# Value projection for two head pairs per pass, 512 weight columns into four PSUM banks, in a transformer block on one Trainium2 core

## The chip, the core and the metric

The kernel runs on one core of one Trainium2 chip, as one launch. Its time is the device time of an execution in microseconds (us). Five engines work side by side, each through its own instruction stream in a fixed order: TensorE (PE, matrix products into the PSUM banks; its weight loads are shown apart as PEld), VectorE (DVE), ScalarE (ACT), GpSimd (POOL) and SyncE (SP, which issues DMA transfers here). A wait between engines is a wait on a semaphore. PSUM is used here as eight banks, each of 512 float32 numbers in each of 128 partitions.

## The reference

One transformer block on x with 512 rows of 2048 float32 numbers:

```
h    = rmsnorm(x, g_attn)
proj = h @ w_in                    # 2048 x 6152: q, k, v of 8 + 8 heads of width 128, and 8 forget logits
o_sb  = stick_breaking_attention(8 heads, strictly causal)
o_fox = forgetting_attention(8 heads, causal softmax with a cumulative log-forget bias)
x = x + concat(head_rmsnorm(o_sb), head_rmsnorm(o_fox)) @ w_out
x = x + relu(rmsnorm(x) @ w_up)**2 @ w_down
y = rmsnorm(x)
```

The change touches only how the values v (two times 8 heads of 128 columns of `proj`) are projected and where some temporaries of the head norm of the second last head and of the last head lie.

## The kernel before, in words

**Three products for one.** Every float32 operand is split into a rounded high part and the remainder: `split` (L57) lets ACT write the high part (L59, or L62 with a scale) and DVE the low part (L60, L63). `mm3` (L82 to L85) then does three PE matmuls for each product: high times high, high times low, low times high.

**Weights.** `load_w` (L70) brings a tile of 1024 columns per partition (512 KB) from HBM by one DMA on SP's queue (L73), into one of three `wraw` buffers, and splits it with one ACT cast (L59) and one DVE subtraction (L60) into `wh` and `wl`, three buffers of each.

**Order of the heads.** `order` holds the heads in pairs: forgetting ("fox") heads 6, 7, then 0 to 5, then stick-breaking ("sb") heads 0 to 7. The loop over n = 0, 2, ..., 14 takes one pair each time. It projects q and k of both heads (`project_q`: 48 matmuls of 512 columns each into one bank of the pool `acc`, tile `accq`), then, from n = 2 on, the values of the pair (`accumulate_v`), and then it attends with both heads. The values of the first pair come out of the stage before, together with the forget logits (264 columns).

**Values.** `accumulate_v` (L152) holds the normalized input hH/hL still (128 rows of x by 128 channels) and moves the weight columns past it. For a pair these are m = 256 columns, so that two of the four row groups t share a bank of 512: two `accv` banks of the pool `acc`, which has four. A weight tile holds four groups of 128 channels (there are 16, counted by k); for each t and each k there are three matmuls 256 columns wide: 16 x 4 x 3 = 192 for a pair. `take_v` (L172) scales and splits the sums into `vh` and `vl`: for each t one ACT (L62) and one DVE instruction (L63) of 128x256.

**Attention.** PSUM gives three banks to the tile `s`/`pt` and one to `o`, `ck`, `ssq`, both single, so heads follow one another. A fox head: `ck` (a matmul, L271) and its ACT copy `cb`, scores `s` on PE, additions into `w` on DVE (L277), causal mask on POOL, row maxima on DVE (L282), Exp on ACT (L285), scaling on DVE (L288), then `pt`: ten PE transposes of `w` (L218). `weigh` (L213) splits `pt` into `ph` and `pl` (one buffer of each), multiplies them with the values into `o`, and takes the norm over the head width: the square sum goes through PE (`ssq`), the rest through DVE and ACT, with `ph` and `pl` again as scratch (`n1`, `n2`); the result is written to `mixed` (L251). The next head's `ph` and `pl` have to wait until the norm of the head before has ended. The last head (`last=True`) has six scratch tiles of its own (`os_last`, `sq_last`, ...) and its `o` and square sum (`oq`) in the three-bank tile.

**After the attention.** The output projection (`acco`, its transposes in L424) goes over the heads in the same order of pairs, k0 = 0 to 14, in four blocks of 512 output columns with four banks each, so that the pair of the last two heads is what its first block needs last. Then come the up and down projections (`accu`, `accd`), which the change leaves as they are.

**Who sets the order.** The program text is rearranged by a scheduler: each engine gets one fixed list of instructions, with the attention of a head at high priority and the projections as what fills PE between its steps. So the order of the changed kernel can be read before it has run.

Of the kernel before, what the change touches and what calls it, by code (L numbers as in the profile page):

```python
# [8 lines left out]
F32 = mybir.dt.float32  # L9
F32R = mybir.dt.float32r  # L10
# [4 lines left out]
P = 128  # L15
NT = 512
TB = NT // P
D = 2048
KC = D // P
NH = 8  # L20
# [16 lines left out]
def block_kernel(ctx, tc, x, g_attn, w_in, b_f, g_out_sb, g_out_fox, w_out, g_mlp, w_up, w_down, g_final, y):  # L37
    nc = tc.nc
    pe, act, dve, pool, sp = nc.tensor, nc.scalar, nc.vector, nc.gpsimd, nc.sync
# [3 lines left out]
    w_in, w_out, w_up, w_down = w_in[0], w_out[0], w_up[0], w_down[0]  # L43
# [9 lines left out]
    acc = ctx.enter_context(tc.tile_pool(name="acc", bufs=4, space=PSUM))  # L53
# [3 lines left out]
    def split(hi, lo, src, scale=None):  # L57
        if scale is None:
            ins = act.copy(hi, src)  # L59
            lows[0] = dve.tensor_tensor(lo, src, hi.bitcast(F32), op=ALU.subtract)  # L60
        else:
            ins = act.mul(hi, src, scale)  # L62
            dve.scalar_tensor_tensor(lo, src, scale, hi.bitcast(F32), op0=ALU.mult, op1=ALU.subtract)  # L63
        return ins
# [5 lines left out]
    def load_w(src, a, b):  # L70

        raw = wp.tile([P, a, b], F32, tag="wraw", name="wraw")
        sp.dma_start(raw, src)  # L73
        out = []
        per = min(a, 2 * NT // b)
        for i in range(0, a, per):
            hi, lo = (w.rearrange("p (a b) -> p a b", a=per) for w in hi_lo(per * b))
            split(hi, lo, raw[:, i:i + per, :])
            out += [(hi[:, j, :], lo[:, j, :]) for j in range(per)]
        return out  # L80
# [42 lines left out]
    g_up, g_sb, g_fx = g_rest[:, :KC], g_rest[:, KC:KC + NH], g_rest[:, KC + NH:]  # L123
# [10 lines left out]
    with (  # L134
# [17 lines left out]
        def accumulate_v(c0, m, steps, prepare=None, more=None):  # L152

            per = NT // m
            banks = [acc.tile([P, NT], F32, tag="acc", name="accv") for _ in range(2)]
            if more is not None:
                banks += [more.tile([P, NT], F32, tag="more", name="accm") for _ in range(2)]
            ps = [banks[t // per][:, t % per * m:(t % per + 1) * m] for t in range(TB)]
            k1 = 0
            for step in steps:  # L160
                k0, k1 = k1, k1 + step
                if prepare is not None:
                    prepare(k0, step)
                w = load_w(w_in[k0 * P:(k0 + step) * P, c0:c0 + m].rearrange("(a p) c -> p a c", p=P), step, m)
                for t in range(TB):
                    ts = slice(t * P, (t + 1) * P)
                    for i in range(step):
                        k = k0 + i
                        mm3(ps[t], hH[:, k, ts], hL[:, k, ts], *w[i], k == 0 and t % per == 0, k == KC - 1)
            return ps  # L170

        def take_v(ps):  # L172
            vh = at.tile([P, TB, 2 * P], F32R, tag="vh", name="vh", bufs=2)
            vl = at.tile([P, TB, 2 * P], F32R, tag="vl", name="vl", bufs=2)
            for t in range(TB):
                split(vh[:, t, :], vl[:, t, :], ps[t][:, :2 * P], r1[:, t:t + 1])
            return vh, vl

        def project_q(c0, c, rb):
            ps = acc.tile([P, NT], F32, tag="acc", name="accq")  # L180
# [12 lines left out]
        def wide(name, dt=F32):  # L193
            return at.tile([P, 1280], dt, tag=name, name=name)
# [9 lines left out]
        def rows(w):  # L204
            return [w[:, OFF_Q[i]:OFF_Q[i] + (i + 1) * P] for i in range(TB)]
# [4 lines left out]
                pool.affine_select(out=d, in_=d, compare_op=op, fill=fill, base=0,  # L210
                                   pattern=[[0, n], [-1, P]] if n > 1 else [[-1, P]], channel_multiplier=1)

        def weigh(h, v, hc, w, gv, last=False):  # L213

            pt = atp.tile([P, 1536], F32, tag="s", name="pt")
            for j in range(TB):
                for i in range(j, TB):
                    pe.transpose(pt[:, OFF_T[j] + (i - j) * P:OFF_T[j] + (i - j + 1) * P],  # L218
                                 w[:, OFF_Q[i] + j * P:OFF_Q[i] + (j + 1) * P], ident)
            ph, pl = wide("ph", F32R), wide("pl", F32R)  # L220
            split(ph, pl, pt[:, :1280])
            hs = slice(hc * P, (hc + 1) * P)
            if last:
                oq = atp.tile([P, 1536], F32, tag="s", name="oq")
                o, q = oq[:, :NT], oq[:, NT:2 * NT]
            else:
                o = atp.tile([P, NT], F32, tag="o", name="o")
            for j in range(TB):
                n = NT - j * P
                js = slice(OFF_T[j], OFF_T[j] + n)  # L230
                mm3(o[:, j * P:], v[0][:, j, hs], v[1][:, j, hs], ph[:, js], pl[:, js], j == 0, j == TB - 1)
            if last:
                os_, sq, va, ra = (at.tile([P, NT], F32, name=f"{c}_last") for c in ("os", "sq", "va", "ra"))
                sh, sl = (at.tile([P, NT], F32R, name=f"{c}_last") for c in ("sh", "sl"))
            else:
                os_ = up.tile([P, NT], F32, tag="ul4", name="os")
                ra = up.tile([P, NT], F32, tag="uh5", name="ra")
                n1, n2 = wide("ph"), wide("pl", F32R)
                sq, va = n1[:, :NT], n1[:, NT:2 * NT]
                sh, sl = n2[:, :NT], n2[:, NT:2 * NT]  # L240
                q = None
            act.copy(os_, o)
            dve.tensor_tensor(sq, os_, os_, op=ALU.mult)
            split(sh, sl, sq)
            if q is None:
                q = atp.tile([P, NT], F32, tag="o", name="ssq")
            pe.matmul(q, onesr, sh, start=True, stop=False)
            pe.matmul(q, onesr, sl, start=False, stop=True)
            dve.tensor_scalar(va, q, 1.0 / P, EPS, op0=ALU.mult, op1=ALU.add)
            rsqrt(va, va, ra, sq)  # L250
            dve.scalar_tensor_tensor(mixed[:, h, :], os_, gv, va, op0=ALU.mult, op1=ALU.mult)  # L251

        def attend_sb(h, v, hc, q, k):
            s = scores(q, k)
            w = wide("w")
            act.activation(w, s, AF.Abs)
            act.activation(w, w, AF.Exp, scale=-1.0)
            act.activation(w, w, AF.Ln, bias=1.0)
            dve.scalar_tensor_tensor(w, s, 0.0, w, op0=ALU.max, op1=ALU.add)
            causal(w, ALU.is_gt, 0.0)  # L260
            for r in rows(w):

                dve.tensor_tensor_scan(r[:, ::-1], r[:, ::-1], r[:, ::-1], 0.0, op0=ALU.add, op1=ALU.max)
            dve.tensor_tensor(w, s, w, op=ALU.subtract)
            act.activation(w, w, AF.Exp)
            causal(w, ALU.is_gt, 0.0)
            weigh(h, v, hc, w, g_sb[:, h:h + 1], h == order[-1])

        def attend_fox(h, v, hc, q, k):
            ck = atp.tile([P, NT], F32, tag="o", name="ck")  # L270
# [21 lines left out]
        order = [NH + h for h in (6, 7, 0, 1, 2, 3, 4, 5)] + list(range(NH))  # L292

        def v_columns(h):
            return 2 * WSB + h * P if h < NH else o0 + 2 * WSB + (h - NH) * P

        with tc.tile_pool(name="tr0", bufs=2, space=PSUM) as trp:
# [30 lines left out]
                            junk = wide("ph")[:, :2 * NT].rearrange("p (a b) -> p a b", a=2)  # L328
                            act.activation(junk, xb[:, c:c + 2, t, :], AF.Square, accum_out=ss1[:, t, k // 8:k // 8 + 1])

            ps = accumulate_v(v_columns(order[0]), 2 * P + NH, [1, 1] + [2] * 7, prepare, trp)
            column_vectors(g_rest, *(g[0].rearrange("(h p) -> h p", p=P) for g in (g_mlp, g_out_sb, g_out_fox)))
            act.dma_start(bf, b_f.to_broadcast([P, NH]))
            r1 = row_rstd(ss1, "r1")
# [22 lines left out]
        with tc.tile_pool(name="attp", bufs=1, space=PSUM) as atp:  # L357
# [6 lines left out]
            fe = at.tile([P, TB, NH], F32, name="fe")  # L364
            for t in range(TB):
                dve.scalar_tensor_tensor(fl[:, t, :], ps[t][:, 2 * P:], r1[:, t:t + 1], bf, op0=ALU.mult, op1=ALU.add)
            v = take_v(ps)
            act.activation(fe, fl, AF.Abs)
            act.activation(fe, fe, AF.Exp, scale=-1.0)
            act.activation(fe, fe, AF.Ln, bias=1.0)  # L370
# [18 lines left out]
            for n in range(0, 2 * NH, 2):  # L389
                def project(i):  # L390
                    h = order[n + i]
                    e = (o0 if h >= NH else 0) + h % NH * P
                    return project_q(e, 2 * i, rbq), project_q(e + WSB, 2 * i + 1, rb)

                def attend(i, qk):
                    h = order[n + i]
                    with tc.high_priority():
                        (attend_fox if h >= NH else attend_sb)(h % NH, v, i, *qk)

                qk = [project(0), project(1)]  # L400
                if n:
                    v = take_v(accumulate_v(v_columns(order[n]), 2 * P, [4] * 4))
                for i in range(2):
                    attend(i, qk[i])

# [7 lines left out]
    trp = trp_cm.__enter__()  # L413
# [14 lines left out]
    for n in range(4):  # L428
        ns = slice(n * NT, (n + 1) * NT)
        ps = [acc.tile([P, NT], F32, tag="acc", name="acco") for _ in range(TB)]  # L430
        for k0 in range(0, 2 * NH, 2):
            e0 = order[k0]
            w = load_w(w_out[e0 * P:(e0 + 2) * P, ns].rearrange("(a p) c -> p a c", p=P), 2, NT)
# [141 lines left out]
    for g in range(NG):  # L575
        for db in range(2):
# [5 lines left out]
            b = load_b(g, db)  # L582
            for j, p in enumerate(ORDER):
                if j in steps:
                    job.step()
                w = b_form(p, b)
# [89 lines left out]
    banks = [(acc, "acc"), (tps, "tps")]  # L676
# [39 lines left out]
```

## Time and profile before

| | |
|---|---|
| median of 3 runs | 2152.41 us (2151.77 to 2153.89) |
| the profiled execution: its time | 2151.46 us |
| the profiled execution: its span (first to last instruction) | 2149.4 us |
| busy PE, PEld, DVE, ACT, POOL | 2131.2, 1801.0, 1402.8, 881.0, 63.2 us |
| granted TensorE clock over the span | 0.998 |

The profile shows one execution. Lines such as L83 are lines of the kernel before. A group row gives line, engine, operation, written tile <- read tiles, shapes and count, then busy time, the mean duration of one in ns, and the idle time of the engine ahead of them with what ended most of it. Matmuls overlap: one of 512 columns is shown as some 390 ns long while the next starts after some 230 ns, so a time for PE is taken from start to start (called the pitch here) and not from the duration. A timeline row gives start and duration in us; in square brackets stands the idle time of the engine before it and what ended that. A window row gives the length of the stretch and the busy time of the engines in it with the count of instructions.

### The profile page before, as it was taken

How to read it: one execution, taken by the hardware profiler on the slowest of the kernel's cores; microseconds unless marked ns; L12 is line 12 of the kernel's file. 1: busy time of each engine (PE TensorE's matmuls, PEld its weight loads, DVE VectorE, ACT ScalarE, POOL GpSimd, SP SyncE). 2: the span in 40 equal slices, each digit the busy share in tenths (PEclk: the TensorE clock that was granted, in tenths of full speed). 3: DMA queues.
4: the chain of work that ended last, by engine and by line, in shares of the span. 5: the costliest groups of instructions: out<-in, count | busy, mean ns of one | idle time of the engine just before them, and what ended most of it. 6: DMA issues, size and time to landing. Idle time of an engine off the chain costs nothing.

```text
span 2149.4 us, 25658 instructions
## 1 busy us (share of the span) xinstructions
PE 2131.2 (99%) x10356; PEld 1801.0 (84%) x10356; DVE 1402.8 (65%) x1547; ACT 881.0 (41%) x1146; POOL 63.2 (3%) x75
## 2 busy tenths in 40 slices
PE   9999999999999999999999999999999999999997
PEld 8888988998997888888888888888888888888886
DVE  5455555766566554566776776766776776777788
ACT  6333333444345445443433333333433433433444
POOL 0000000000010000000000000000000000000005
PEclk9999999999999999999999999999999999999999
DMA  6333333322333324233333233233233233233323
GB/s 189 80 84 83 78 83 84 79 79 79 89 112 123 94 93 157 69 118 98 98 114 102 89 117 108 89 114 112 88 108 118 88 99 120 87 101 120 92 70 127
DMA packets 201366, 216.71 MB, mean 101 GB/s; under 512 B 6768, under 2 KB 156832, under 8 KB 201120
## 3 DMA queue, kind: packets, MB, share of 16 engines
q1 hardware_dynamic: 200288, 212.95, 32.9%
q10 hardware_dynamic: 960, 2.13, 0.3%
q8 instruction: 81, 1.33, 0.3%
q14 instruction: 37, 0.30, 0.0%
HBM read 210.86 MB, written 4.19 MB: 100 GB/s over the span
## 4 chain that ended last, share of the span: by engine, by line
PE 96%; DVE 2%; ACT 1%; DMA 1%; issue 0%; POOL 0%; SPq 0%; ACTq 0%; DVEq 0%
PE accu L83 11%; PE accu L84 11%; PE accu L85 11%; PE accd L85 9%; PE accd L83 9%; PE accd L84 9%; PE accq L85 5%; PE accq L83 5%; PE accq L84 5%; PE acco L83 3%; PE acco L84 3%; PE accv L83 3%; PE accv L85 3%; PE acco L85 3%; PE accv L84 3%; PE pt L218 1%
## 5 line engine op out<-in xcount | busy, mean ns | idle before, releaser
L59 ACT CAST wh<-wraw 128x1024 fp32r<-128x1024 f32 (+2 forms) x261 | 270.0, 1035 | 409.9 <-PE accd L85 153.7
L60 DVE TENSOR_TENSOR wl<-wraw,wh 128x1024 fp32r<-128x1024 f32 (+2 forms) x261 | 314.3, 1205 | 166.1 <-ACT wh L59 133.7
L564 DVE TENSOR_TENSOR m<-m,accd 128x1024 f32<-128x1024 f32 x204 | 248.7, 1219 | 263.4 <-PE accd L85 261.7
L83 PE MATMUL accu<-h2h,wh 128*128 128x512 f32 x1024 | 398.6, 389 | 0.0
L84 PE MATMUL accu<-h2l,wh 128*128 128x512 f32 x1024 | 398.4, 389 | 0.0
L85 PE MATMUL accu<-h2h,wl 128*128 128x512 f32 x1024 | 383.7, 389 | 0.0
L59 ACT CAST wh<-wd 128x1024 fp32r<-128x1024 f32 x210 | 219.6, 1052 | 273.6 <-PE accd L85 151.1
L83 PE MATMUL accd<-wh,ufh 128*128 128x512 f32 x840 | 326.8, 389 | 0.0
L84 PE MATMUL accd<-wl,ufh 128*128 128x512 f32 x840 | 326.8, 389 | 0.0
L85 PE MATMUL accd<-wh,ufl 128*128 128x512 f32 x840 | 326.8, 389 | 0.0
L60 DVE TENSOR_TENSOR wl<-wd,wh 128x1024 fp32r<-128x1024 f32 x210 | 255.1, 1221 | 15.1 <-ACT wh L59 13.8
L83 PEld LDWEIGHTS accu<-h2h,wh 128*128 128x128 f32 x1024 | 192.2, 188 | 39.9
L84 PEld LDWEIGHTS accu<-h2l,wh 128*128 128x128 f32 x1024 | 192.2, 188 | 39.8
L85 PEld LDWEIGHTS accu<-h2h,wl 128*128 128x128 f32 x1024 | 192.1, 188 | 39.9
L85 PE MATMUL accq<-hH,wl 128*128 128x512 f32 x512 | 200.8, 392 | 0.0
L83 PE MATMUL accq<-hH,wh 128*128 128x512 f32 x512 | 200.6, 392 | 0.0
L84 PE MATMUL accq<-hL,wh 128*128 128x512 f32 x512 | 200.4, 391 | 0.0
L84 PEld LDWEIGHTS accd<-wl,ufh 128*128 128x128 f32 x840 | 157.7, 188 | 32.8
L85 PEld LDWEIGHTS accd<-wh,ufl 128*128 128x128 f32 x840 | 157.6, 188 | 32.7
L83 PEld LDWEIGHTS accd<-wh,ufh 128*128 128x128 f32 x840 | 157.6, 188 | 32.7
L83 PE MATMUL accv<-wh,hH 128*128 128x256 f32 (+1 forms) x480 | 137.4, 288 | 0.7 <-ACT hH L62 0.7
L84 PE MATMUL accv<-wl,hH 128*128 128x256 f32 (+1 forms) x480 | 135.5, 284 | 0.0
(213 smaller groups left out, 2736.7 us busy)
## 6 DMA issues: line engine op xcount, KB each, us to landing
wraw<-in_w_up_dram SPq DMA_DIRECT2D x128, 512.0 KB, 3.7
wd<-in_w_down_dram SPq DMA_DIRECT2D x120, 512.0 KB, 3.6
wraw<-in_w_in_dram SPq DMA_DIRECT2D x92, 512.0 KB, 3.7
wraw<-in_w_out_dram SPq DMA_DIRECT2D x32, 512.0 KB, 3.6
m<-in_x_dram SPq DMA_DIRECT2D x4, 1024.0 KB, 11.9
wraw<-in_w_down_dram SPq DMA_DIRECT2D x8, 512.0 KB, 4.2
mixed<-in_x_dram SPq DMA_DIRECT2D x2, 1024.0 KB, 10.8
wraw<-in_w_in_dram SPq DMA_DIRECT2D x7, 264.0 KB, 6.8
```

The lines of the kernel that those rows point to most:

```text
L59: ins = act.copy(hi, src)
L60: lows[0] = dve.tensor_tensor(lo, src, hi.bitcast(F32), op=ALU.subtract)
L83: pe.matmul(out, sh, mh, start=first, stop=False, skip_group_check=True)
L84: pe.matmul(out, sh, ml, start=False, stop=False, skip_group_check=True)
L85: pe.matmul(out, sl, mh, start=False, stop=last, skip_group_check=True)
L218: pe.transpose(pt[:, OFF_T[j] + (i - j) * P:OFF_T[j] + (i - j + 1) * P], w[:, OFF_Q[i] + j * P:OFF_Q[i] + (j + 1) * P], ident)
L564: dve.tensor_tensor(M[p][:, :, db, :], M[p][:, :, db, :], ps, op=ALU.add)
```

## The change

`accumulate_v` takes a list of column starts and may cover two pairs of heads at once: m = 512 columns, four `accv` banks (all of the pool `acc`), two groups of 128 channels for each weight tile, so a tile still has 1024 columns. This is done at n = 2 (for the pairs of n = 2 and 4), n = 6 (for 6 and 8) and n = 10 (for 10 and 12). At n = 4, 8 and 12 the values are there already. The pair of n = 14 keeps its 256 columns. At n = 6 the two pairs are fox heads 4, 5 and sb heads 0, 1, whose columns don't lie side by side, so each weight tile is loaded by two DMAs of half its size. `take_v` splits two pairs: for each t two ACT and two DVE instructions of 128x256. The value tiles `vh`, `vl` get three buffers instead of two. The head norm of the second last head (`left == 1`) uses one buffer each of `vh` and `vl` as scratch instead of `ph` and `pl`; the last head (`left == 0`) uses `ph` and `pl` as the others do, and four of its own scratch tiles go.

```diff
     def load_w(src, a, b):
         raw = wp.tile([P, a, b], F32, tag="wraw", name="wraw")
-        sp.dma_start(raw, src)
+        src = src if isinstance(src, list) else [src]
+        for i, r in enumerate(src):
+            n = b // len(src)
+            sp.dma_start(raw[:, :, i * n:(i + 1) * n], r)
...
         def accumulate_v(c0, m, steps, prepare=None, more=None):
             per = NT // m
-            banks = [acc.tile([P, NT], F32, tag="acc", name="accv") for _ in range(2)]
+            banks = [acc.tile([P, NT], F32, tag="acc", name="accv") for _ in range(2 if more is not None else TB // per)]
...
-                w = load_w(w_in[k0 * P:(k0 + step) * P, c0:c0 + m].rearrange("(a p) c -> p a c", p=P), step, m)
+                w = load_w([w_in[k0 * P:(k0 + step) * P, c:c + m // len(c0)].rearrange("(a p) c -> p a c", p=P) for c in c0],
+                           step, m)
...
-        def take_v(ps):
-            vh = at.tile([P, TB, 2 * P], F32R, tag="vh", name="vh", bufs=2)
-            vl = at.tile([P, TB, 2 * P], F32R, tag="vl", name="vl", bufs=2)
+        def take_v(ps, pairs=1):
+            vs = [tuple(at.tile([P, TB, 2 * P], F32R, tag=f"v{c}", name=f"v{c}", bufs=3) for c in "hl") for _ in range(pairs)]
             for t in range(TB):
-                split(vh[:, t, :], vl[:, t, :], ps[t][:, :2 * P], r1[:, t:t + 1])
-            return vh, vl
+                for i, (vh, vl) in enumerate(vs):
+                    split(vh[:, t, :], vl[:, t, :], ps[t][:, i * 2 * P:(i + 1) * 2 * P], r1[:, t:t + 1])
+            return vs
...
-        def weigh(h, v, hc, w, gv, last=False):
+        def weigh(h, v, hc, w, gv, left=2):
...
-            if last:
+            if left == 0:
                 oq = atp.tile([P, 1536], F32, tag="s", name="oq")
...
-            if last:
-                os_, sq, va, ra = (at.tile([P, NT], F32, name=f"{c}_last") for c in ("os", "sq", "va", "ra"))
-                sh, sl = (at.tile([P, NT], F32R, name=f"{c}_last") for c in ("sh", "sl"))
+            if left == 0:
+                os_, ra = (at.tile([P, NT], F32, name=f"{c}_last") for c in ("os", "ra"))
             else:
                 os_ = up.tile([P, NT], F32, tag="ul4", name="os")
                 ra = up.tile([P, NT], F32, tag="uh5", name="ra")
+            if left == 1:
+                n1 = at.tile([P, 2 * NT], F32, tag="vh", name="n1", bufs=3)
+                n2 = at.tile([P, 2 * NT], F32R, tag="vl", name="n2", bufs=3)
+            else:
                 n1, n2 = wide("ph"), wide("pl", F32R)
-                sq, va = n1[:, :NT], n1[:, NT:2 * NT]
-                sh, sl = n2[:, :NT], n2[:, NT:2 * NT]
-                q = None
+            sq, va = n1[:, :NT], n1[:, NT:2 * NT]
+            sh, sl = n2[:, :NT], n2[:, NT:2 * NT]
...
-            weigh(h, v, hc, w, g_sb[:, h:h + 1], h == order[-1])
+            weigh(h, v, hc, w, g_sb[:, h:h + 1], NH - 1 - h)
...
-                if n:
-                    v = take_v(accumulate_v(v_columns(order[n]), 2 * P, [4] * 4))
+                if n == 2 * NH - 2:
+                    vs = take_v(accumulate_v([v_columns(order[n])], 2 * P, [4] * 4))
+                elif n % 4 == 2:
+                    c = [v_columns(order[n + i]) for i in (0, 2)]
+                    vs = take_v(accumulate_v(c[:1] if c[1] == c[0] + 2 * P else c, 4 * P, [2] * 8), 2)
+                v = vs.pop(0)
```

## The prediction on record

> **What bounds the kernel now.** First the page: busy time of the engines and the chain that ended last.
>
> ```profile
> span 2149.4 us, 25658 instructions
> ...
> PE 2131.2 (99%) x10356; PEld 1801.0 (84%) x10356; DVE 1402.8 (65%) x1547; ACT 881.0 (41%) x1146; POOL 63.2 (3%) x75
> ...
> PE 96%; DVE 2%; ACT 1%; DMA 1%; issue 0%; POOL 0%; SPq 0%; ACTq 0%; DVEq 0%
> ```
>
> PE is busy for all but 18 us and carries 96% of the chain. So the time is the sum of PE's pitches plus its few waits, and any other engine counts only where PE waits for it. Next the windows of the late attention and of the passage to the output projection, and PE's waits, longest first.
>
> ```profile
> 380.00:630.00 250.00, 250.00 (x1512) 224.71 (x1511) 154.99 (x179) 111.78 (x128) 19.05 (x29) 1.00 0.30 81
> 660.00:720.00 60.00, 57.83 (x265) 47.55 (x265) 36.47 (x48) 30.76 (x47) 0.00 (x0) 1.00 0.30 88
> ```
>
> ```profile
> PE trg L300 <- DMA g_rows<-in_g_attn_dram: 3.2, 1, 3.2
> PE acco L83 <- ACT uh L59: 2.1, 1, 2.1
> ```
>
> In the 250 us of attention PE never idles: the projections fill every gap, at a granted clock of 1.00. The only wait of PE that the change can reach is the one of 2.1 us in the second window, where the output projection waits for the last head. So three things count: pitch, this wait, and new waits.
>
> **Part 1: half as many matmuls, twice as wide.** The matmuls of the values, and two of them 18 starts apart:
>
> ```profile
> L83 PE MATMUL accv<-wh,hH 128*128 128x256 f32 x448 | 127.5, 285 | 0.0
> ```
>
> ```profile
> 157.75 0.28 PE L83 MATMUL accv<-wh,hH 128*128 128x256 f32 x1
> ...
> 159.91 0.28 PE L83 MATMUL accv<-wh,hH 128*128 128x256 f32 x1
> ```
>
> L84 and L85 have the same count, 1344 in all, 192 for each of seven pairs. Pitch: (159.91 - 157.75) / 18 = 0.120 us. Six of the seven pairs now go in three passes of 16 k x 4 t x 3 = 192 matmuls of 512 columns: 576 wide ones take the place of 1152. No wide `accv` exists yet. The nearest is `acco`, which also holds activations still and moves 512 weight columns; `accq` has the same width with the operands changed over. 33 starts of PE in a stretch of `acco`, and 9 of `accq`:
>
> ```profile
> 675.79 0.39 PE L84 MATMUL acco<-wl,uh 128*128 128x512 f32 x1
> ...
> 683.27 0.39 PE L85 MATMUL acco<-wh,ul 128*128 128x512 f32 x1
> 685.73 0.50 PE L83 MATMUL acco<-wh,uh 128*128 128x512 f32 x1 [2.07 <-ACT uh L59]
> ```
>
> ```profile
> 113.59 0.39 PE L85 MATMUL accq<-hH,wl 128*128 128x512 f32 x1
> ...
> 115.65 0.39 PE L85 MATMUL accq<-hH,wl 128*128 128x512 f32 x1
> ```
>
> 7.48 / 33 = 0.2267 us and 2.06 / 9 = 0.2289 us. So a pair of narrow ones costs 0.240 and its successor 0.2267 to 0.2289: 11 to 13 ns saved, 576 times: 6.4 to 7.6 us. I take **7.0 us**. The same numbers of columns move; what goes is a fixed part of each matmul of 11 to 13 ns.
>
> The Trainium skill (TensorE: Matmul & The Clock Gate, Back-to-back issue gap) gives the warm gap as N/2.4 + 2.5 ns: by it the fixed part would be 2.5 ns, and the saving 576 x 2.5 ns = 1.4 us, an estimate from that page. The rows disagree (it gives 109 and 216 ns where they show 120 and 227); they decide here.
>
> **Part 2: the last heads.** The chain of waits around the end of attention:
>
> ```profile
> 638.31 1.09 PE pt L218 x10
> ...
> 653.63 0.23 PE ssq L248
> ...
> 668.60 0.23 PE oq L83
> ...
> 677.77 0.23 PE oq L248
> ...
> 684.28 0.76 DVE mixed L251
> 685.06 0.63 ACT uh L59
> ```
>
> The last head's transposes end at 639.4, but its product with the values (`oq`) starts only at 668.6: `ph` and `pl` serve the norm of the head before, whose square sum ends at 653.9. So the last result is late, and PE waits 2.07 us at 685.73. With the scratch of the second last head in a spare value buffer this dependence is gone. The order of instructions of the changed kernel, which can be read before it has run, puts all twelve `oq` products before the last `ssq`, and 83 `acco` matmuls between the last `oq` and the first that needs the last pair: 83 x 0.2267 = 18.8 us. From the last `oq` to the split result the rows show 685.69 - 678.00 = 7.7 us. Cover: 11 us, so the wait goes: **2.1 us** saved. Next late there is nothing: what follows is the sums into `m` and the transposes, behind which `acco` of the next block fills, as before. If the cover is gone, 0. The third value buffer is idle by then; the last head now uses `ph`/`pl` as scratch, with nobody behind it.
>
> **Part 3: new waits.** `accv` now takes all four banks of `acc`, so what follows on PE needs `take_v` first. Its instructions and those of a weight tile:
>
> ```profile
> L62 ACT ACTIVATE vh<-accv,r1v x30: 457/475/486, 50.9 to 638.3; 128x256 fp32r<-128x256 f32 x30
> L63 DVE SCALAR_TENSOR_TENSOR vl<-accv,r1v,vh x30: 454/483/486, 52.2 to 639.5; 128x256 fp32r<-128x256 f32 x30
> ```
>
> ```profile
> L59 ACT CAST wh<-wraw 128x1024 fp32r<-128x1024 f32 (+2 forms) x261 | 270.0, 1035 | 409.9 <-PE accd L85 153.7
> L60 DVE TENSOR_TENSOR wl<-wraw,wh 128x1024 fp32r<-128x1024 f32 (+2 forms) x261 | 314.3, 1205 | 166.1 <-ACT wh L59 133.7
> ...
> wraw<-in_w_in_dram SPq DMA_DIRECT2D x92, 512.0 KB, 3.7
> ```
>
> In the last step of a pass the four banks end 6 matmuls (1.37 us) apart, so the first ends 4.1 us before the last. The changed order has ACT do t0 and t1 of the first pair, then of the second. Bank 0 is free after t1's end (1.37 + 0.39), two casts (0.95) and one DVE half (0.48), 3.2 us after its last matmul, and `o` or `pt` matmuls (1.1 us) stand on PE between the pass and the next `accq`, which so comes 5.2 us after it. So at n = 2 and n = 10, where both engines come straight to the splits, **0** (if ACT or DVE is late, the delay less 2.0 us). At its start a pass finds three banks emptied early; the fourth is first used 5.5 us or more of PE work after the first.
>
> At **n = 6** the order is another. After the pass stand the transposes `pt` of a fox head whose `ck` comes only 41 `accv` matmuls earlier: 41 x 0.228, and `ck` itself 0.49 as the rows below show it, are 9.8 us. (The other fox heads have 14.4 to 15.7 us of PE work there, those of the kernel before at least 13.4.) What that chain needs, twice, from `ck` to the last scaling of `w`:
>
> ```profile
> 151.12 0.49 PE L271 MATMUL ck<-ckT,nsel 16*128 16x512 f32 x1
> ...
> 305.38 0.49 PE L271 MATMUL ck<-ckT,nsel 16*128 16x512 f32 x1
> ```
>
> ```profile
> 161.19 1.28 DVE L288 TENSOR_SCALAR w<-w,ml 128x128 f32<-128x128 f32 x4
> ...
> 317.00 1.27 DVE L288 TENSOR_SCALAR w<-w,ml 128x128 f32<-128x128 f32 x4
> ```
>
> ```profile
> 158.65 0.40 ACT L285 ACTIVATE w<-w,ml 128x128 f32<-128x128 f32 x1 [2.89 <-DVE ml L283]
> ...
> 314.46 0.40 ACT L285 ACTIVATE w<-w,ml 128x128 f32<-128x128 f32 x1 [1.43 <-DVE ml L283]
> ```
>
> 162.47 - 151.12 = 11.4 us and 318.27 - 305.38 = 12.9 us. So PE waits 1.6 to 3.1 us. On ACT two value casts now stand before the four Exp, the second waiting for t1 of the pass: 0.49 + 29 x 0.228 + 0.39 + 0.48 = 8.0 us after `ck`, where Exp started 7.5 and 9.1 us after it; that adds at most 0.5. Behind Exp on ACT are the other casts, needed by `accq` only after the 1.1 us of `pt`. I take **2.5 us**; ends 0 (chain faster with less beside it) and 5 (casts and DVE halves also in the way).
>
> The rest costs nothing. Splits, casts and loaded bytes are as many as before. A weight tile now lasts 24 x 0.228 = 5.5 us on PE, not 5.8, against 1.0 us of ACT, 1.2 of DVE and 3.7 of landing, with three buffers. On SP's queue the pass at n = 6 issues 16 loads of half the size, each pair behind one wait for a buffer; queued behind them are only later weight tiles. Without this cover a late tile would cost up to 3.7 us once. The values of a first head come some 20 us later after its scores, which PE covers with `accv` itself; the order leaves each other chain about as much PE work as before (scores to `pt` of sb heads 18 us, where 15.8 went without a wait).
>
> **Sum.** -7.0 - 2.1 + 2.5 = -6.6 us. Own execution: 2151.46 - 6.6 = 2144.9; the median lies 0.95 us above it, so 2152.41 - 6.6 = **2145.8**.
>
> **Rivals.** (a) *No wait at n = 6*: 2152.4 - 9.1 = 2143.3. For it: chains vary by 1.5 us. Against: even the shorter is over 9.8. (b) *A further wait of 1.5 to 6 us*, after a pass or from a late weight tile: 2147.3 to 2151.8. For it: ACT and DVE take their lists strictly in order, and PE no longer has a spare bank. Against: no PE wait in 250 us before. (c) *The 11 to 13 ns belong to the columns of `accv`, not to the instruction*, so wide ones take 0.240: only parts 2 and 3 are left, 2152.8. Against: `acco`, of the same form, has 0.2267. The rule of the Trainium skill (TensorE: Matmul & The Clock Gate, Back-to-back issue gap) comes out near it: with its 1.4 us, 2151.4, an estimate from that page. (d) *Slower: four banks bind.* If the eight splits only begin when the pass has ended, PE stands 8 x 0.475 + 0.48 = 4.3 us at n = 2 and n = 10 and 6.8 at n = 6, 15.4 in all: 2152.4 - 9.1 + 15.4 = 2158.7. It makes the kernel slower once these waits sum to more than 9.1 us. Against: ACT is busy only 112 of 250 us, and the banks end staggered. That the change doesn't happen is excluded: the changed order has 576 wide and 192 narrow `accv`.
>
> **How the numbers follow.** Forecast 0.58, (a) 0.12, (b) 0.16, (c) 0.07, (d) 0.07. A measurement of this kernel tells about 0.2% (4.3 us) from no change, so faster means below 2148.1: the forecast, (a) and a quarter of (b), 0.74; within: the rest of (b) and (c), 0.19; slower: (d), 0.07. Range: from 2142.5 (part 1 at 7.6, part 2 whole, no new wait, 0.2 of scatter) to 2151.0 (into (b)); outside lie (d), (c) and the end of (b).
>
> **What would show it.** Wide `accv` about 0.227 us apart; PE's wait for the last head gone from the list; one new wait, `pt` for DVE `w`, 1.6 to 3.1 us near 340 us; no idle PE at the ends of the other two passes. `accq` waiting for `vl` would show (b) or (d), wide `accv` at 0.24 would show (c), and a wait of `acco` for `uh` that stays would refute part 2.

## The result, and the profile after

| | before | after |
|---|---|---|
| median | 2152.10 us (2151.77 to 2153.89, 4 runs) | 2142.98 us (2142.21 to 2144.17, 4 runs) |
| ratio | | 0.9954, 95% interval 0.9942 to 0.9965 |
| profiled execution: time, span | 2151.46, 2149.4 us | 2144.17, 2142.2 us |

The change is faster by 9.1 us (median against median), 0.46% by the ratio; 6.6 us were forecast. The two profiled executions are only 7.3 us apart. The page after, busy times and chain:

```profile
span 2142.2 us, 24535 instructions
...
PE 2124.3 (99%) x9780; PEld 1770.8 (83%) x9780; DVE 1401.6 (65%) x1547; ACT 877.1 (41%) x1146; POOL 60.8 (3%) x75
...
PE 96%; DVE 1%; ACT 1%; DMA 1%; issue 0%; POOL 0%; ACTq 0%; DVEq 0%
```

PE has 10356 - 9780 = 576 matmuls fewer and is the bound as before. Its waits after:

```profile
PE trg L306 <- DMA g_rows<-in_g_attn_dram: 3.2, 1, 3.2
PE tr L152 <- DVE nsel L361: 2.1, 1, 2.1
PE accv L86 <- ACT hH L62: 0.7, 2, 0.5
PE pt L222 <- DVE w L294: 0.6, 1, 0.6
```

`acco` no longer waits for `uh`. Two rows are new: `pt` for `w`, the one that was forecast at n = 6, and `tr` for 2.1 us in the first 7 us of the kernel, where no instruction has changed. DVE's `nsel` is named there because it came last among what the profile shows. To place such a row, the time is cut at landmarks that both kernels have, read from PE's timeline. They are the first matmul of the value pass of n = 2, the first `acco`, the first `accu` and PE's last matmul; each column gives the time from the landmark before it:

| us | start to first value pass | to first `acco` | to first `accu` | to last matmul |
|---|---|---|---|---|
| before | 141.93 | 494.82 | 188.65 | 1313.05 |
| after | 143.59 | 488.68 | 185.90 | 1313.06 |
| difference | +1.66 | -6.14 | -2.75 | +0.01 |

So the change brought 8.9 us, and 1.66 us went the other way in a stage that it doesn't touch; 1.25 us of these are there by the first `accv` of the kernel, at 6.37 us before and 7.62 after. The attention stage gives 6.14 us, the passage to the output projection 2.75 us.

The wide matmuls, by groups and 21 starts apart in the pass of n = 2:

```profile
L86 PE MATMUL accv<-wh,hH 128*128 128x512 f32 x192 | 75.1, 391 | 0.0
...
L86 PE MATMUL accv<-wh,hH 128*128 128x256 f32 x64 | 18.2, 284 | 0.0
```

```profile
185.83 0.39 PE L86 MATMUL accv<-wh,hH 128*128 128x512 f32 x1
...
190.59 0.39 PE L86 MATMUL accv<-wh,hH 128*128 128x512 f32 x1
```

4.76 / 21 = 0.2267 us, the pitch of `acco` to four digits. The ends of two wide passes on PE's timeline, first n = 6, then n = 10:

```profile
342.96 0.39 PE L88 MATMUL accv<-wh,hL 128*128 128x512 f32 x1
343.92 1.97 PE L222 MATMUL pt<-ident,w 128*128 128x128 f32 x10 [0.56 <-DVE w L294]
345.64 0.48 PE L86 MATMUL accq<-hH,wh 128*128 128x512 f32 x1
```

```profile
500.31 0.39 PE L88 MATMUL accv<-wh,hL 128*128 128x512 f32 x1
500.54 1.25 PE L222 MATMUL pt<-ident,w 128*128 128x128 f32 x10
501.55 0.48 PE L86 MATMUL o<-ph,vh 128*128 128x512 f32 x1
```

From the last `accv` over the ten transposes to the next matmul PE takes 1.24 us at n = 10 and 2.68 us at n = 6: the wait costs 1.44 us there, though its row says 0.6. The row counts from the shown end of the last matmul (0.39 long, 0.23 apart) and leaves out that the transposes then started by and by, as the four scalings ended (1.97 us for the ten, where n = 10 has 1.25). What they waited for, on PE and DVE:

```profile
333.34 0.50 PE L277 MATMUL ck<-ckT,nsel 16*128 16x512 f32 x1
```

```profile
343.36 0.18 DVE L292 RECIPROCAL ml<-ml 128x4 f32<-128x4 f32 x1 [1.70 <-ACT w L291]
343.57 1.27 DVE L294 TENSOR_SCALAR w<-w,ml 128x128 f32<-128x128 f32 x4
```

The last scaling ends 344.84 - 333.34 = 11.5 us after `ck`, within the 11.4 to 12.9 us of before. PE's first transpose starts at 343.92, when the first of the four scalings is done. At the end of the pass of n = 2, `accq` takes its bank without a wait:

```profile
191.04 0.39 PE L88 MATMUL accv<-wh,hL 128*128 128x512 f32 x1
191.27 0.39 PE L86 MATMUL o<-ph,vh 128*128 128x512 f32 x1
...
192.47 0.40 PE L86 MATMUL accq<-hH,wh 128*128 128x512 f32 x1
```

And the last heads, in the chain that ended last, with DVE's row of the result:

```profile
639.67 1.11 PE pt L222 x10
648.19 0.23 PE oq L86
...
651.25 0.23 PE ssq L254
...
657.37 0.23 PE oq L254
```

```profile
664.14 0.75 DVE L257 SCALAR_TENSOR_TENSOR mixed<-os_last,g_rest,ph 128x512 f32<-128x512 f32 x1
```

`oq` now comes 7.4 us behind the last head's transposes (29 before) and ahead of the end of `ssq`, and the result is there at 664.89. The first matmul that needs the last pair starts at 676.24, 11 us later; with the 0.6 us of the split between them that is near the cover that was forecast.

### The profile page after: what moved, and what is told of

It is laid out like the page before. It is cut to its first block, busy times and chain, and to the rows that moved or that the text cites. A ratio compares the mean times of both kernels' runs of the same rounds, so it can differ in the third digit from the quotient of the medians.

```text
span 2142.2 us, 24535 instructions
## 1 busy us (share of the span) xinstructions
PE 2124.3 (99%) x9780; PEld 1770.8 (83%) x9780; DVE 1401.6 (65%) x1547; ACT 877.1 (41%) x1146; POOL 60.8 (3%) x75
## 4 chain that ended last, share of the span: by engine, by line
PE 96%; DVE 1%; ACT 1%; DMA 1%; issue 0%; POOL 0%; ACTq 0%; DVEq 0%
PE accu L86 11%; PE accu L88 11%; PE accu L87 11%; PE accd L87 9%; PE accd L88 9%; PE accd L86 9%; PE accq L86 5%; PE accq L88 5%; PE accq L87 5%; PE acco L88 3%; PE acco L86 3%; PE acco L87 3%; PE accv L86 3%; PE accv L87 3%; PE accv L88 3%; PE pt L222 1%
## 5 line engine op out<-in xcount | busy, mean ns | idle before, releaser
L59 ACT CAST ufh<-c 128x512 fp32r<-128x512 f32 x75 | 46.5, 623 | 191.3 <-PE accd L87 191.1
L87 PEld LDWEIGHTS accq<-hL,wh 128*128 128x128 f32 x512 | 96.2, 188 | 19.9 <-issue 0.5
```

The costliest lines, as they stand in the source:

```text
L87: pe.matmul(out, sh, ml, start=False, stop=False, skip_group_check=True)
```

## The experiments

Theory: the change acts through three things, each in its own place: a fixed part of some 13 ns in each matmul of the values, a wait of 1.44 us at n = 6, and the wait for the last heads. Rivals: the gain lies in the form of the pass (banks, weight tiles) and not in the count of matmuls; the wait for the last heads went because of the wide passes; the start got slower by the change. These landmarks are from each run's own profile:

| us | start to first value pass | to first `acco` | to first `accu` | to last matmul |
|---|---|---|---|---|
| the change once more | 141.79 | 488.67 | 185.90 | 1313.06 |
| wide passes alone | 143.16 | 488.72 | 188.58 | 1313.06 |
| scratch alone | 143.18 | 494.82 | 185.96 | 1313.06 |
| halves | 142.07 | 494.53 | 185.97 | 1313.07 |
| pass of n = 6 moved | 143.32 | 487.22 | 185.91 | 1313.06 |
| before, second profile | 143.60 | 494.81 | 189.90 | 1313.07 |
| before, third | 142.74 | 494.82 | 190.08 | 1313.09 |
| before, fourth | 142.57 | 494.81 | 188.65 | 1313.07 |
| before, fifth | 142.39 | 494.82 | 188.65 | 1313.05 |

**The change once more**, no edit.

> The changed kernel once more, to see how much of the 9 us lies in the start of single executions. Its profiled execution lost 1.66 us in the first 34 us against the profile of before, and was the slowest of four. Theory (scatter of the first loads): some executions have this and some not, on both sides, and the median stays 8.9 us below before (-7.6 wide matmuls, +1.4 wait at n = 6, -2.7 last heads). Rival (the change itself slows the start): all executions start 1.7 us later and the median is 7.2 us below.

Measured: 2142.89 us (5 runs), before 2153.88 (21 runs on that chip), ratio 0.9950 (0.9938 to 0.9963). The start took 141.79 us, the other stages were the same to 0.01 us. So the 1.66 us are scatter of the start, which lay between 141.8 and 143.6 us on both sides in all profiles. But before's 21 runs were 1.8 us slower in the median than the four above, and that was not expected: 9 of them lie from 2151.6 to 2152.7 and 12 from 2153.6 to 2154.9. The last four rows of the table take this up.

**Wide passes alone**: the scratch of the second last head back in `ph` and `pl`.

```diff
-            if left == 1:
+            if left > 2:
                 n1 = at.tile([P, 2 * NT], F32, tag="vh", name="n1", bufs=3)
```

> The changed kernel with the scratch of the second last head back in ph and pl. Theory (the parts add): the last heads' wait of PE of some 2.1 us comes back, time 6.1 us below before (-7.6 + 1.4), that is 2.7 above the whole change. Rival (the wide passes or the third value buffer took the wait away): as the whole change, 8.9 us below, without a wait of acco for uh.

Measured: 2146.33 us (5 runs), ratio 0.9968 (0.9956 to 0.9981), 3.4 us above the change (its profiled start took 1.4 us longer). The attention stage is that of the change (488.72), the passage that of before (188.58), and so is the wait:

```profile
PE acco L86 <- ACT uh L59: 2.1, 1, 2.1
```

**Scratch alone**: values projected narrowly for each pair, all else as in the change.

```diff
-                if n == 2 * NH - 2:
+                if n:
                     vs = take_v(accumulate_v([v_columns(order[n])], 2 * P, [4] * 4))
-                elif n % 4 == 2:
-                    c = [v_columns(order[n + i]) for i in (0, 2)]
-                    vs = take_v(accumulate_v(c[:1] if c[1] == c[0] + 2 * P else c, 4 * P, [2] * 8), 2)
```

> The kernel before with three value buffers and the scratch of the second last head in the spare one; values projected narrowly for each pair. Theory: PE's wait of acco for uh goes, 2.1 to 2.8 us below before. Rival (it goes only because the wide passes leave ACT and DVE more room): no change, 0.

Measured: 2149.80 us (11 runs), ratio 0.9982 (0.9973 to 0.9991). Attention as before (494.82), passage as after (185.96): 2.7 us, and PE's wait is gone. The two halves of the change add up (6.1 + 2.7 = 8.8 of 8.9 us), each in its own stage. The rival is out: the wait falls with the scratch, whatever the passes.

**Halves**: the change, with each wide matmul issued as two of 256 columns.

```diff
-                        mm3(ps[t], hH[:, k, ts], hL[:, k, ts], *w[i], k == 0 and t % per == 0, k == KC - 1)
+                        for c in range(0, m, 2 * P) if m == NT else (None,):
+                            cs = slice(None) if c is None else slice(c, c + 2 * P)
+                            mm3(ps[t][:, cs], hH[:, k, ts], hL[:, k, ts], w[i][0][:, cs], w[i][1][:, cs],
+                                k == 0 and t % per == 0 and not c, k == KC - 1)
```

> The changed kernel with each wide matmul of the values issued as two of 256 columns on the halves of the same bank: same loads, same four banks, same splits, only 576 matmuls more. Theory (each matmul has a fixed part of some 13 ns): 576 x 0.0131 = 7.5 us slower than the whole change in the passes; its order leaves 14 us between ck and pt at n = 6, so the wait of 1.4 us there goes: 6.1 us slower in sum. Rival (the gain lies in the weight tiles and banks of the wide pass, not in the count of matmuls): as fast as the whole change or up to 1.4 us faster.

Measured: 2149.03 us (11 runs), 6.1 above the change; in the attention stage 494.53 - 488.67 = 5.86 us. Its list of PE's waits has no `pt`, as expected, so this is the gain of the count less the 1.44 us of that wait. With the same loads, banks and casts the gain is gone with the count. 24 starts in its pass of n = 2:

```profile
160.05 0.28 PE L86 MATMUL accv<-wh,hH 128*128 128x256 f32 x1
...
162.93 0.28 PE L86 MATMUL accv<-wh,hH 128*128 128x256 f32 x1
```

2.88 / 24 = 0.120 us, as before.

**Quarters**: the same with four of 128 columns.

```diff
+                        for c in range(0, m, P) if m == NT else (None,):
+                            cs = slice(None) if c is None else slice(c, c + P)
```

> The changed kernel with each wide matmul of the values issued as four of 128 columns on quarters of the same bank. Theory (a fixed part of 13 ns beside 0.417 ns for each column, from 0.1199 and 0.2267 us for 256 and 512): 0.0665 us apart, 576 x (0.266 - 0.2267) = 23 us above the change. Rival (a weight load has a pitch of its own that a matmul cannot go below, and 0.12 us at 256 columns is near it): some 0.11 us apart, as the 128 columns of pt have some 0.1, 576 x (0.44 - 0.2267) = 123 us above.

Measured: 2267.51 us (one execution), 124.5 above the change. 33 starts:

```profile
152.31 0.28 PE L88 MATMUL accv<-wh,hL 128*128 128x128 f32 x1
...
155.99 0.28 PE L88 MATMUL accv<-wh,hL 128*128 128x128 f32 x1
```

3.68 / 33 = 0.1115 us, where the theory gave 0.0665: the rival holds at 128 columns. So 0.0133 + 0.000417 N us, a line through the pitches of 256 and 512 columns, doesn't reach down to 128, and 256 lies just above the floor (0.120 against 0.112). The change's own profile shows what keeps this distance, where scores of 384 and of 128 columns follow one another (PEld is a weight load):

```profile
233.60 0.33 PE L86 MATMUL s<-uh 128*128 128x384 f32 x1
...
234.13 0.23 PE L86 MATMUL s<-uh 128*128 128x128 f32 x1
234.13 0.19 PEld L87 LDWEIGHTS s<-ul,uh 128*128 128x128 f32 x1
234.19 0.28 PE L87 MATMUL s<-ul,uh 128*128 128x128 f32 x1
234.24 0.19 PEld L88 LDWEIGHTS s<-uh,ul 128*128 128x128 f32 x1
234.30 0.27 PE L88 MATMUL s<-uh,ul 128*128 128x128 f32 x1
234.35 0.19 PEld L86 LDWEIGHTS s<-uh 128*128 128x128 f32 x1
```

The three matmuls of 384 columns take 0.53 / 3 = 0.177 us each (0.173 by the line). Of those of 128 the second starts 0.06 us after the first, as the line has it (0.067), and the third only 0.11 us after the second: its load comes 0.11 us behind the load before, at 234.24, and the matmul 0.06 us after its load. So in these rows it is the loads that keep 0.11 us between them, and in the run with quarters they come 0.11 us apart too. The Trainium skill (TensorE: Matmul & The Clock Gate, LDWEIGHTS (loading the stationary operand)) gives a weight load as columns / 1.2 ns, by which 128 columns take 107 ns, an estimate from that page; the 111.5 ns here are near it.

**Pass of n = 6 moved** between the projections of its two heads.

```diff
-                qk = [project(0), project(1)]
+                qk = [project(0)]
+                if n != 6:
+                    qk.append(project(1))
...
+                if n == 6:
+                    qk.append(project(1))
                 v = vs.pop(0)
```

> The changed kernel with the wide pass of n = 6 put between the projections of its first and its second head, so that no transposes wait at its end: at least 13.8 us of PE work then stand between ck and pt of every fox head. Theory (the pass's end met a softmax not yet done, which cost PE 1.44 us from start to start): the stretch from the first value pass to the first acco takes 487.2 us instead of 488.67, the median is 1.4 us below that of the change run before (2142.9), so 2141.5. Rival (the casts of the two pairs are late wherever the pass ends, since all four banks are taken): the wait comes back as accq waiting for vl, and the time stays at 2142.9.

Measured: attention stage 487.22 us, 1.45 below the change, to 0.02 us what was expected. The list of PE's waits has no `pt` left, and no `accq` in its place:

```profile
PE trg L306 <- DMA g_rows<-in_g_attn_dram: 3.2, 1, 3.2
PE tr L152 <- DMA mixed<-in_x_dram: 1.5, 2, 1.3
PE accv L86 <- ACT hH L62: 0.7, 2, 0.5
PE acce L87 <- DVE wll L60: 0.5, 1, 0.5
```

The median, 2142.64 us (2141.40 to 2142.91, 5 runs; ratio 0.9952, 0.9938 to 0.9965), doesn't show 1.4 us against 2142.89: its profiled start was 143.32 us, that of the change 141.79. By its stages it is the best version, 10.3 us below before; by medians the two can't be told apart.

**Before, four more profiles**, no edit; the first:

> The kernel before, profiled once more. Theory (single executions differ only in the first loads): from the first value pass on all stages have the same length to 0.1 us (494.82 us to the first acco, 188.65 to the first accu, 1313.05 to the last matmul), and only the start of the first value pass moves, from 141.9 us by 0 to 3. Rival (the scatter comes from DMA or clock all along the kernel): the difference is spread over the stages.

The start moved as expected, but the passage took 189.90 us instead of 188.65: a miss. The wait for the last head is the same (2.46 us from start to start). Behind it, from 1.4 us after its end, the granted clock (the column after the counts) is halved for 3.4 us. The windows 689 to 691 us of this profile, and of the fourth, whose passage took 188.65:

```profile
689.00:691.00 2.00, 2.00 (x6) 0.50 0.07 26
```

```profile
689.00:691.00 2.00, 1.90 (x11) 1.00 0.00 0
```

> The kernel before, profiled again for the length of its passage to the output projection, which took 188.65 us in one profiled execution and 189.90 in another. Theory (PE's wait of 2.46 us from start to start for the last head sometimes lowers the granted clock for some 3 us after it): either 188.65 with a clock of 1.00 behind the wait, or about 189.9 with 0.50 there; nothing between. Rival (loads late by chance): other lengths, with waits for a load.

> As the run before it: the kernel before, once more, 188.65 or about 189.9 us for the passage by the theory of the clock.

> As the two runs before it: the kernel before, once more, 188.65 or about 189.9 us for the passage by the theory of the clock.

Measured: passages of 190.08, 188.65 and 188.65 us, with a clock of 0.50 behind the wait in the first and 1.00 in the two others. So in two of five executions the passage took 1.25 to 1.43 us more, with the clock halved right behind the wait. None of the six profiles of versions without this wait has such a drop; nor has that of wide passes alone, which keeps the wait. What makes the clock fall in one execution and not in the next stays open. The Trainium skill (TensorE: Matmul & The Clock Gate, Why this matters for your kernels) says "No PE-idle gaps >~3µs between matmul bursts"; here a gap of 2.46 us was enough in two of five.

## Why the prediction was right or wrong

The direction and all three places were right, and no fourth wait came. The size was not: 8.9 us by the stages where the sum said 6.6. All terms erred to the same side, by 0.6, 0.6 and 1.1 us.

- **Part 1, 7.0 us: measured 7.6** (6.14 + 1.45 of the wait, shown by the run with the pass moved). The clean rows alone gave it: 2 x 0.1200 - 0.2267 = 13.3 ns, 576 times 7.7. The step that failed was to go half way to `accq`: its nine starts stood right behind a `ck`, and mixed the cost of a break in the stream into the pitch of a width. The rival of the columns is out: one matmul of 512 columns takes 13 ns less than two of 256. The 2.5 ns of the Trainium skill (TensorE: Matmul & The Clock Gate, Back-to-back issue gap), which that page gives for an isolated matmul, don't hold in these streams.
- **Part 2, 2.1 us: measured 2.7 to 2.75**, shown by wide passes and scratch alone. The mechanism and the 11 us of cover held. The step that failed took the idle time from the wait's row; from start to start PE lost 2.46 - 0.23 = 2.23 us, and 0.5 us more in the matmuls and transposes right behind it. The lowered clock that follows the wait in some executions, 1.25 us or more, no row of the one profile could show.
- **Part 3, wait at n = 6, 2.5 us: measured 1.44**, the largest error. Its place and its releaser were right, and so were the 9.8 us of PE work in front of it. The step that failed in the main was the length of the chain from `ck` to the last scaling: 2.5 us stands for some 12.3, and it took 11.5, near the shorter of the two that were read off, which gives 1.7. The rest, 0.3 us, is that the transposes didn't wait for the last scaling: the first starts 0.9 us ahead of its end. At n = 2 and n = 10 zero was right, and rival (d) with its four banks found no wait.
- **The comparison.** The forecast started from 2152.41 us. Before falls into two groups some 2 us apart. The two profiled executions with the lowered clock took 2154.37 and 2153.72 us and lie in the upper group, the three others (2151.46 to 2152.09) in the lower. Of the 30 runs of before beside the later versions, six have a mean granted clock of 0.997, all in the upper group; so has the longest run of wide passes alone (2148.97 us, 2.6 above the median), which keeps the wait, and none of the runs without the wait. So the drop of the clock is likely what parts the groups, with the scatter of the start on top; that is argued, not shown. It also means that the 8.9 us of the stages are the gain over an execution without the drop, and that where before has it the change saves 1.25 to 1.43 us more. Why the start takes 141.8 to 143.6 us was not tried; in most profiles PE's waits there name the first loads of x.

## What to carry to other kernels

Where one engine is the bound, take pitches from start to start in a stretch without breaks, for the old and the new width alike, and price a wait the same way; the idle time in a row counts from a shown end and is too small. To find what a change did, lay landmarks that both kernels have beside each other: here undisturbed stages agreed to 0.1 us where whole times scattered by 3. A wait of the bounding engine can be worth more than its length where its clock drops behind it, so one profile is not enough to price it.

## What the runs showed of the hardware

- In an unbroken stream, each with a weight load of its own, matmuls of these operands start 0.2267 us apart at 512 columns, 0.120 at 256 and 0.1115 at 128. The first two fit 13 ns and 0.417 ns a column; at 128 the weight loads, 0.11 us apart, set the pace, while a single matmul of 128 columns can start 0.06 us after the one before.
- The second matmul behind a group of transposes comes late: in the change's pass of n = 10 it started 0.31 us after the first `accv` instead of 0.227.

```profile
472.33 1.25 PE L222 MATMUL pt<-ident,w 128*128 128x128 f32 x10
473.34 0.48 PE L86 MATMUL accv<-wh,hH 128*128 128x512 f32 x1
473.65 0.39 PE L87 MATMUL accv<-wl,hH 128*128 128x512 f32 x1
```

- A gap of 2.46 us between starts on PE was followed by a granted clock of 0.50 for 3.4 us in two of five executions of the same kernel.
